# Stationary halves at 14 turns of placement and pass order, in the transposed projections of a decoder trunk

## The chip, the core and the metric

One core of one Trainium2 chip runs the whole kernel. The metric is device microseconds (us) of one execution, from the runs' own times. Before the change the median of two runs is 2431.1 us (2430.3 to 2431.9).

## What is computed

A two-layer decoder trunk on one sequence of 256 tokens with width 2048, in float32: a retention layer, a gated ConvFFN, a sliding-window attention layer, a second ConvFFN, and a last RMSNorm. The reference, cut to its order:

```python
def reference(x, ...):
    h = x
    for i in range(DEPTH):                      # DEPTH = 2
        j = i // N_MIXERS
        hn = rmsnorm(h, norm_mix_g[i])
        if i % N_MIXERS == 0:
            h = h + retention(hn, ret_w_in[j], ret_w_out[j])
        else:
            h = h + sliding_window_attention(hn, att_w_qkv[j], att_b_qkv[j], att_sinks[j], att_w_out[j])
        hn = rmsnorm(h, norm_ffn_g[i])
        h = h + conv_ffn(hn, ffn_w_up[i], ffn_conv_w[i], ffn_conv_b[i], ffn_w_down[i])
    return rmsnorm(h, final_norm_g)
```

Nearly all of the work is `hn @ w` with weights that are read once from HBM: 456 MB of them.

## The kernel before, in words

**Weights come in units.** A unit (`Unit`) is one transfer of 1 MB: up to 2048 words in each of the 128 partitions, for instance 8 chunks of 128 weight rows by 256 columns, or 4 chunks by 512. SP issues the transfers into `raw` (L146 in the printed functions below), some units ahead. ACT rounds `raw` to the high half `hi` (L161), VectorE subtracts to get the low half `lo` (L162), both in pieces of 1024 words. `hi` and `lo` have four buffers each, and each buffer is 2048 + 64 words long, so that the data may start up to 64 words into it. A product of a weight and an activation is built from three products of halves: high by high, high by low and low by high.

**Two kinds of product.** In the output projections and the values (`products`, L256 to L258), the weights are the moving operand and the activations the stationary one: three passes of 512 columns (256 in one unit kind) into the same PSUM tile, each with its own 128 by 128 stationary tile. In the transposed projections (`products_tr`, L267 and L269: queries, keys, and the up projections of both FFNs), the weights are stationary. One *chunk* there is four passes: the stationary tiles H0 and H1 (the two 128-column halves of `hi`) are each applied to the moving tile `xT` in 512 columns (high and low half of the activations side by side), then L0 and L1 (of `lo`) are each applied to the first 256 columns of the same tile. H0 and L0 add into PSUM bank 0 of the group, H1 and L1 into bank 1. Sixteen chunks (2048 rows) make a group, which is then evicted.

**Passes and loads.** Each pass needs its stationary tile loaded (LDWEIGHTS, shown as PEld) before it begins; the load of a pass runs while the pass before it streams its moving tile. A pass of 512 columns is a long cover for the next load, a pass of 256 columns a short one.

**Where the tiles lie.** All `xT` tiles and all `hi`/`lo` buffers start at multiples of 64 words (256 bytes). In units that have a transposed group, `hi` and `lo` start `ASIDE` = 48 words into their buffers, in the others at 0. So the distance from the start of the moving tile to the start of the tile that is being loaded is, modulo 64 words, 48 for every load in a transposed group. In the `products` units it is 0, and 16 in the three units that hold the attention's keys and values together (moving at 48, stationary at 0).

**Order.** `run_main` goes over the units, and in a unit over groups and chunks; after each chunk it lets the splits run ahead (`split_ahead`) and runs pending small tasks (evictions, scores, transposes), whose PE instructions then stand between chunks. PE executes in the order written.

Of the kernel before, what the change touches and what calls it, by code (L numbers as in the profile page):

```python
# [10 lines left out]
F32R = mybir.dt.float32r  # L11
# [5 lines left out]
P = 128  # L17
D = 2048
S = 256
# [12 lines left out]
AHEAD = 3  # L32
# [13 lines left out]
RAW = 2  # L46
SPLIT = 1024

ASIDE = 48
F_CUTS = [0, 14, 28, NF]  # L50
START = (1, 1, 2, 2, 2)

# [57 lines left out]
class Kernel:  # L110
# [37 lines left out]
    def splits(self, i):  # L148

        u = self.units[i]  # L150
        nc = self.nc
        w = u.n * u.cols
        at = ASIDE if any(g.tr for g in u.groups) else 0
        u.hi, u.lo = (
            self.wp.tile([P, 2048 + 64], F32R, tag=tag, name=tag, bufs=AHEAD + 1)[:, at : at + w]
            for tag in ("hi", "lo")
        )
        for c in range(0, w, SPLIT):
            e = min(c + SPLIT, w)
            raw, hi, lo = (x[:, c:e] for x in (u.raw, u.hi, u.lo))  # L160
            nc.scalar.copy(out=hi, in_=raw)  # L161
            nc.vector.tensor_tensor(out=lo, in0=raw, in1=hi.bitcast(F32), op=ALU.subtract)  # L162
            yield e / w
# [29 lines left out]
    def run_main(self):  # L193
        for i, u in enumerate(self.units):
            self.load_to(i + AHEAD + RAW)
            self.split_ahead(i)
            for g in u.groups:
                if g.ps is None:
                    if g.begin:
                        g.begin()  # L200
                    g.ps = self.banks(g)
            if u.groups[0].by_token:
                break
            for j, g in enumerate(u.groups):
                c0 = sum(x.cols for x in u.groups[:j])
                for kk, ch in enumerate(u.chunks):
                    sl = slice(kk * u.cols + c0, kk * u.cols + c0 + g.cols)
                    if g.tr:
                        self.products_tr(g, u.hi[:, sl], u.lo[:, sl], u.act[ch])
                    else:  # L210
                        for t in range(2):
                            out = g.ps[t] if g.apart else g.ps[:, t]
                            self.products(g, out, t, u.hi[:, sl], u.lo[:, sl], u.act[ch])
                    g.seen += 1
                    self.step += g.cols / 512
                    if g.seen == g.total:
                        g.done(g)
                    share = (self.step - u.at) / u.steps
                    self.split_ahead(i, share - 1e-6)
                    self.run_tasks()  # L220
        self.run_by_token(self.units[i:])
        while self.tasks:
            self.step += 1
            self.run_tasks()
# [32 lines left out]
        nc.tensor.matmul(out, lhsT=ah, rhs=lo, start=False, stop=False)  # L257
        nc.tensor.matmul(out, lhsT=al, rhs=hi, start=False, stop=last)  # L258

    def products_tr(self, g, hi, lo, act):  # L260

        nc = self.nc
        first, last = g.seen == 0, g.seen == g.total - 1
        both = act.rearrange("p x s -> p (x s)")
        tiles = [(g.ps[:, i], slice(i * P, (i + 1) * P)) for i in range(2)]
        for out, sl in tiles:
            nc.tensor.matmul(out, lhsT=hi[:, sl], rhs=both, start=first, stop=False)  # L267
        for out, sl in tiles:
            nc.tensor.matmul(  # L269
                out[:, :S], lhsT=lo[:, sl], rhs=act[:, 0], start=False, stop=last  # L270
            )


    def transposes(self, ps, ins):
# [683 lines left out]
```

## Time and profile before

| | before |
|---|---|
| median of the runs | 2431.1 us |
| the profiled execution's own time | 2431.45 us |
| its span, first to last instruction | 2429.3 us |
| PE busy | 2413.0 us (99%) |
| weight loads (PEld) busy | 2060.6 us (85%) |
| VectorE busy | 1554.9 us (64%) |
| ScalarE busy | 1224.6 us (50%) |
| mean granted TensorE clock | 0.999 |
| mean DMA rate | 189 GB/s |

Busy times of PE are unions of overlapping instructions: a pass of 512 columns lasts 393 ns from its first to its modelled last moment, but the next one starts long before that. What a pass costs is therefore read from starts: the start of the next pass minus its own start. The timeline view merges equal instructions that follow each other into one row with xN, so that a row "L267 ... x2" followed by "L269 ... x2" shows when the H pair and the L pair began.

### The profile page before, as it was taken

How to read it: one execution, taken by the hardware profiler on the slowest of the kernel's cores; microseconds unless marked ns; L12 is line 12 of the kernel's file. 1: busy time of each engine (PE TensorE's matmuls, PEld its weight loads, DVE VectorE, ACT ScalarE, POOL GpSimd, SP SyncE). 2: the span in 40 equal slices, each digit the busy share in tenths (PEclk: the TensorE clock that was granted, in tenths of full speed). 3: DMA queues.
4: the chain of work that ended last, by engine and by line, in shares of the span. 5: the costliest groups of instructions: out<-in, count | busy, mean ns of one | idle time of the engine just before them, and what ended most of it. 6: DMA issues, size and time to landing. Idle time of an engine off the chain costs nothing.

```text
span 2429.3 us, 31370 instructions
## 1 busy us (share of the span) xinstructions
PE 2413.0 (99%) x12676; PEld 2060.6 (85%) x12676; DVE 1554.9 (64%) x2104; ACT 1224.6 (50%) x1782; POOL 29.2 (1%) x37
## 2 busy tenths in 40 slices
PE   8999999999999999999999999999999999999998
PEld 7888888888888888888888888888888888888887
DVE  6555555554556775677577756876777477657774
ACT  6444344344445553555355545765555355535553
POOL 3000000000000000000000000000000000000000
PEclk9999999999999999999999999999999999999999
DMA  8655555555554555555555555445454555554553
GB/s 287 213 187 180 192 181 186 185 188 182 182 191 168 199 185 194 192 192 183 197 192 195 194 182 195 182 156 193 174 194 174 207 191 191 190 207 175 195 200 126
DMA packets 68977, 460.27 MB, mean 189 GB/s; under 512 B 8032, under 2 KB 9184, under 8 KB 16736
## 3 DMA queue, kind: packets, MB, share of 16 engines
q1 hardware_dynamic: 68544, 457.23, 52.7%
q8 instruction: 99, 1.62, 0.3%
q10 hardware_dynamic: 288, 1.05, 0.1%
q14 instruction: 46, 0.38, 0.0%
HBM read 456.15 MB, written 2.10 MB: 189 GB/s over the span
## 4 chain that ended last, share of the span: by engine, by line
PE 97%; DMA 1%; issue 1%; POOL 0%; DVE 0%; ACT 0%; SPq 0%; POOLq 0%; DVEq 0%; ACTq 0%
PE mm L267 33%; PE mm L269 17%; PE mm L256 13%; PE mm L258 12%; PE mm L257 12%; PE po L256 2%; PE po L258 2%; PE po L257 2%; PE po L393 1%; PE ms L276 1%; PE ms L679 1%; PE ms L503 0%; POOL acc L309 0%; DMA h<-in_xT 0%; DVE lo L162 0%
## 5 line engine op out<-in xcount | busy, mean ns | idle before, releaser
L162 DVE TENSOR_TENSOR lo<-raw,hi 128x1024 fp32r<-128x1024 f32 (+1 forms) x849 | 1018.4, 1219 | 612.3 <-ACT hi L161 611.9
L161 ACT CAST hi<-raw 128x1024 fp32r<-128x1024 f32 (+1 forms) x849 | 857.8, 1042 | 522.5 <-PE mm L258 332.3
L267 PE MATMUL mm<-xT,hi 128*128 128x512 f32 x3552 | 1107.9, 393 | 6.2 <-DVE xT L323 6.2
L269 PEld LDWEIGHTS mm<-xT,lo 128*128 128x128 f32 x3552 | 667.3, 188 | 150.3 <-DVE lo L162 3.1
L269 PE MATMUL mm<-xT,lo 128*128 128x256 f32 x3552 | 702.2, 279 | 1.1 <-DVE lo L162 1.0
L267 PEld LDWEIGHTS mm<-xT,hi 128*128 128x128 f32 x3552 | 540.5, 188 | 11.7 <-ACT hi L161 6.2
L256 PE MATMUL mm<-hi,zT 128*128 128x512 f32 x688 | 268.3, 390 | 0.0
L258 PE MATMUL mm<-hi,zT 128*128 128x512 f32 x688 | 267.7, 389 | 0.0
L257 PE MATMUL mm<-lo,zT 128*128 128x512 f32 x688 | 267.7, 389 | 0.0
L601 DVE SCALAR_TENSOR_TENSOR cv<-u,cw,cv 128x255 f32<-128x255 f32 x344 | 158.3, 481 | 6.1
L256 PE MATMUL mm<-hi,yT 128*128 128x512 f32 x384 | 153.3, 399 | 0.0
L258 PEld LDWEIGHTS mm<-hi,zT 128*128 128x128 f32 x688 | 129.1, 188 | 27.0
L257 PEld LDWEIGHTS mm<-lo,zT 128*128 128x128 f32 x688 | 129.2, 188 | 26.5
L256 PEld LDWEIGHTS mm<-hi,zT 128*128 128x128 f32 x688 | 129.1, 188 | 26.4
L258 PE MATMUL mm<-hi,yT 128*128 128x512 f32 x384 | 149.8, 390 | 0.0
L257 PE MATMUL mm<-lo,yT 128*128 128x512 f32 x384 | 149.7, 390 | 0.0
L378 ACT COPY u<-mm 128x512 f32<-128x512 f32 x86 | 50.4, 586 | 183.7 <-PE mm L269 183.7
L379 DVE TENSOR_TENSOR u<-mm,u 128x512 f32<-128x512 f32 x86 | 59.5, 692 | 93.2 <-ACT u L378 93.2
L594 ACT ACTIVATE cv<-u,cw 128x256 f32<-128x256 f32 x172 | 94.2, 595 | 48.7 <-DVE u L388 48.7
L611 ACT CAST zT<-cv 128x256 fp32r<-128x256 f32 x86 | 34.9, 406 | 156.2 <-DVE cv L609 156.2
L256 PE MATMUL mm<-hi,xT 128*128 128x512 f32 (+1 forms) x288 | 109.1, 379 | 0.0
L258 PE MATMUL mm<-hi,xT 128*128 128x512 f32 (+1 forms) x288 | 108.6, 377 | 0.0
(118 smaller groups left out, 1784.1 us busy)
## 6 DMA issues: line engine op xcount, KB each, us to landing
raw<-in_up SPq DMA_DIRECT2D x172, 1024.0 KB, 4.7
raw<-in_ret_in SPq DMA_DIRECT2D x94, 1024.0 KB, 4.8
raw<-in_dn SPq DMA_DIRECT2D x72, 1024.0 KB, 4.8
raw<-in_ret_out SPq DMA_DIRECT2D x32, 1024.0 KB, 4.7
raw<-in_qkv SPq DMA_DIRECT2D x20, 1024.0 KB, 4.7
raw<-in_att_out SPq DMA_DIRECT2D x14, 1024.0 KB, 4.7
raw<-in_dn SPq DMA_DIRECT2D x16, 512.0 KB, 3.2
raw<-in_dn SPq DMA_DIRECT2D x8, 768.0 KB, 4.3
```

The lines of the kernel that those rows point to most:

```text
L161: nc.scalar.copy(out=hi, in_=raw)
L162: nc.vector.tensor_tensor(out=lo, in0=raw, in1=hi.bitcast(F32), op=ALU.subtract)
L256: nc.tensor.matmul(out, lhsT=ah, rhs=hi, start=first, stop=False)
L257: nc.tensor.matmul(out, lhsT=ah, rhs=lo, start=False, stop=False)
L258: nc.tensor.matmul(out, lhsT=al, rhs=hi, start=False, stop=last)
L267: nc.tensor.matmul(out, lhsT=hi[:, sl], rhs=both, start=first, stop=False)
L269: nc.tensor.matmul(out[:, :S], lhsT=lo[:, sl], rhs=act[:, 0], start=False, stop=last)
L378: nc.scalar.copy(out=x, in_=g.ps[:, :, S:])
L379: nc.vector.tensor_tensor(out=x, in0=g.ps[:, :, :S], in1=x, op=ALU.add)
L594: nc.scalar.activation(out=c[:, half], in_=u[:, half], func=AF.Identity, scale=w[:, 2:3], bias=w[:, 3:4])
L601: nc.vector.scalar_tensor_tensor(out=c[:, half, d:], in0=u[:, half, : S - d], scalar=w[:, 2 - d : 3 - d], in1=c[:, half, d:], op0=ALU.mult ...
L611: nc.scalar.copy(out=z[:, 0], in_=s)
```

## The change

`CASES` holds 14 triples: the offset of `hi` in its buffer, the offset of `lo`, and the order of the four passes. Unit number i takes triple i modulo 14; units without a transposed group keep offset 0 and have no use for the order.

- 7 triples keep `hi` at 48 and put `lo` at 0, 8, 16, 24, 32, 40 or 56.
- 4 keep `lo` at 48 and put `hi` at 0, 16, 32 or 56.
- 3 keep both at 48 and take another order: H0 H1 L1 L0, H0 L0 L1 H1, or H0 L1 L0 H1.

In the first and the last chunk of a group the old order H0 H1 L0 L1 is kept, because these carry the start and stop marks of the accumulation.

```diff
-ASIDE = 48
+CASES = [(48, x, "H0H1L0L1") for x in (0, 8, 16, 24, 32, 40, 56)]
+CASES += [(x, 48, "H0H1L0L1") for x in (0, 16, 32, 56)]
+CASES += [(48, 48, x) for x in ("H0H1L1L0", "H0L0L1H1", "H0L1L0H1")]
...
-        at = ASIDE if any(g.tr for g in u.groups) else 0
+        *at, u.order = CASES[i % len(CASES)]
+        if not any(g.tr for g in u.groups):
+            at = (0, 0)
         u.hi, u.lo = (
-            self.wp.tile([P, 2048 + 64], F32R, tag=tag, name=tag, bufs=AHEAD + 1)[:, at : at + w]
-            for tag in ("hi", "lo")
+            self.wp.tile([P, 2048 + 64], F32R, tag=tag, name=tag, bufs=AHEAD + 1)[:, x : x + w]
+            for tag, x in zip(("hi", "lo"), at)
         )
...
-                        self.products_tr(g, u.hi[:, sl], u.lo[:, sl], u.act[ch])
+                        self.products_tr(g, u.hi[:, sl], u.lo[:, sl], u.act[ch], u.order)
...
-        tiles = [(g.ps[:, i], slice(i * P, (i + 1) * P)) for i in range(2)]
-        for out, sl in tiles:
-            nc.tensor.matmul(out, lhsT=hi[:, sl], rhs=both, start=first, stop=False)
-        for out, sl in tiles:
-            nc.tensor.matmul(
-                out[:, :S], lhsT=lo[:, sl], rhs=act[:, 0], start=False, stop=last
-            )
+        if first or last:
+            order = CASES[0][2]
+        for n in range(0, 8, 2):
+            i = int(order[n + 1])
+            out, sl = g.ps[:, i], slice(i * P, (i + 1) * P)
+            if order[n] == "H":
+                nc.tensor.matmul(out, lhsT=hi[:, sl], rhs=both, start=first, stop=False)
+            else:
+                nc.tensor.matmul(
+                    out[:, :S], lhsT=lo[:, sl], rhs=act[:, 0], start=False, stop=last
+                )
```

What that makes of the loads can be counted in the built program by its addresses. A load is named by the pass that streams meanwhile and the tile that is loaded (HL: an H pass streams, an L tile is loaded), and by the distance of the two modulo 64 words. Before, all of them are at 48.

| load | 0 | 8 | 16 | 24 | 32 | 40 | 48 | 56 | not at 48 |
|---|---|---|---|---|---|---|---|---|---|
| HH (under 512 columns) | 136 | | 136 | | 128 | | 1242 | 128 | 528 |
| HL (under 512 columns) | 118 | 118 | 120 | 132 | 132 | 144 | 868 | 144 | 908 |
| LL (under 256 columns) | 118 | 118 | 120 | 132 | 132 | 144 | 868 | 144 | 908 |
| LH (under 256 columns) | 126 | | 129 | | 120 | | 1212 | 124 | 499 |

The orders show in PE's sequence of instructions. First place: the first unit of the second retention head (early in the program), queries, chunks one to four; `mm` is the PSUM tile, `hi_1085` and `lo_1086` the unit's halves, `po` a retention output that stands between. Before:

```order
L267 MATMUL mm_1178<-xT_118,hi_1085 128x512 x2
L269 MATMUL mm_1178<-xT_118,lo_1086 128x256 x2
L267 MATMUL mm_1178<-xT_120,hi_1085 128x512 x2
L269 MATMUL mm_1178<-xT_120,lo_1086 128x256 x2
L393 MATMUL po_1193<-v_1039,sch_952 128x512 x3
L267 MATMUL mm_1178<-xT_128,hi_1085 128x512 x2
L269 MATMUL mm_1178<-xT_128,lo_1086 128x256 x2
```

The same place after the change (lines 276 and 278 are the H and the L pass there):

```order
L276 MATMUL mm_1178<-xT_118,hi_1085 128x512 x2
L278 MATMUL mm_1178<-xT_118,lo_1086 128x256 x2
L276 MATMUL mm_1178<-xT_120,hi_1085 128x512
L278 MATMUL mm_1178<-xT_120,lo_1086 128x256 x2
L276 MATMUL mm_1178<-xT_120,hi_1085 128x512
L402 MATMUL po_1193<-v_1039,sch_952 128x512 x3
L276 MATMUL mm_1178<-xT_128,hi_1085 128x512
L278 MATMUL mm_1178<-xT_128,lo_1086 128x256 x2
```

From the second chunk on, the two L passes stand between the two H passes; the work between the chunks stays where it was. Second place: a unit of the first FFN's up projection, whose turn is H0 L0 L1 H1, in the middle of it, after the change:

```order
L276 MATMUL mm_5578<-xT_5128,hi_5481 128x512
L278 MATMUL mm_5578<-xT_5128,lo_5482 128x256 x2
L276 MATMUL mm_5578<-xT_5128,hi_5481 128x512
L276 MATMUL mm_5578<-xT_5143,hi_5481 128x512
L278 MATMUL mm_5578<-xT_5143,lo_5482 128x256 x2
L276 MATMUL mm_5578<-xT_5143,hi_5481 128x512
```

The H1 of one chunk and the H0 of the next now follow each other, so that the passes still come in twos: two of 512 columns, two of 256.

## Rows read from the trace of the kernel before

**Rows 1.** The page: span, PE's busy time, granted clock in 40 slices.

```profile
span 2429.3 us, 31370 instructions
...
PE 2413.0 (99%) x12676; PEld 2060.6 (85%) x12676; DVE 1554.9 (64%) x2104; ACT 1224.6 (50%) x1782; POOL 29.2 (1%) x37
...
PEclk9999999999999999999999999999999999999999
```

**Rows 2.** Waits of PE: engine, line, waited for: total us, times, longest.

```profile
PE mm L267 <- DVE xT L323: 6.2, 1, 6.2
PE mm L269 <- DVE lo L162: 1.0, 3, 0.5
PE ms L352 <- POOL acc L309: 0.4, 1, 0.4
```

**Rows 3.** The page's chain that ended last: shares by engine, then by line.

```profile
PE 97%; DMA 1%; issue 1%; POOL 0%; DVE 0%; ACT 0%; SPq 0%; POOLq 0%; DVEq 0%; ACTq 0%
PE mm L267 33%; PE mm L269 17%; PE mm L256 13%; PE mm L258 12%; PE mm L257 12%; PE po L256 2%; PE po L258 2%; PE po L257 2%; PE po L393 1%; PE ms L276 1%; PE ms L679 1%; PE ms L503 0%; POOL acc L309 0%; DMA h<-in_xT 0%; DVE lo L162 0%
```

**Rows 4.** The page's costliest groups: count | busy us, mean ns | idle before.

```profile
L267 PE MATMUL mm<-xT,hi 128*128 128x512 f32 x3552 | 1107.9, 393 | 6.2 <-DVE xT L323 6.2
L269 PEld LDWEIGHTS mm<-xT,lo 128*128 128x128 f32 x3552 | 667.3, 188 | 150.3 <-DVE lo L162 3.1
L269 PE MATMUL mm<-xT,lo 128*128 128x256 f32 x3552 | 702.2, 279 | 1.1 <-DVE lo L162 1.0
```

**Rows 5.** PE's timeline in a steady up projection: start us, us, instruction, count.

```profile
895.16 0.62 PE L267 MATMUL mm<-xT,hi 128*128 128x512 f32 x2
895.62 0.39 PE L269 MATMUL mm<-xT,lo 128*128 128x256 f32 x2
895.85 0.62 PE L267 MATMUL mm<-xT,hi 128*128 128x512 f32 x2
896.30 0.40 PE L269 MATMUL mm<-xT,lo 128*128 128x256 f32 x2
896.54 0.62 PE L267 MATMUL mm<-xT,hi 128*128 128x512 f32 x2
...
904.82 0.62 PE L267 MATMUL mm<-xT,hi 128*128 128x512 f32 x2
```

**Rows 6.** The same in a steady down projection: two starts, 84 passes apart.

```profile
1150.56 0.39 PE L256 MATMUL mm<-hi,zT 128*128 128x512 f32 x1
...
1169.60 0.39 PE L256 MATMUL mm<-hi,zT 128*128 128x512 f32 x1
```

**Rows 7.** Timeline, attention's values: 12 passes of 256 columns, distance 16.

```profile
1465.27 0.28 PE L256 MATMUL mm<-hi,xT 128*128 128x256 f32 x1
...
1466.68 0.60 PE L276 MATMUL ms<-ident,h 128*128 128x128 f32 x4
```

**Rows 8.** Timeline, L pairs before other work: distance 0, 0, 40.

```profile
82.68 0.39 PE L269 MATMUL mm<-xT,lo 128*128 128x256 f32 x2
82.90 0.63 PE L393 MATMUL po<-v,sch 128*128 128x512 f32 x2
...
1136.02 0.40 PE L269 MATMUL mm<-xT,lo 128*128 128x256 f32 x2
1136.26 0.39 PE L256 MATMUL mm<-hi,zT 128*128 128x512 f32 x1
...
753.48 0.41 PE L269 MATMUL mm<-xT,lo 128*128 128x256 f32 x2
753.72 0.60 PE L276 MATMUL ms<-ident,h 128*128 128x128 f32 x4
```

**Rows 9.** Timeline, the first four passes of a down projection.

```profile
905.51 0.40 PE L256 MATMUL mm<-hi,zT 128*128 128x512 f32 x1
...
906.44 0.39 PE L257 MATMUL mm<-lo,zT 128*128 128x512 f32 x1
```

**Rows 10.** Groups by line, 800 to 890 us (offset 48), then 905 to 970 (offset 0).

```profile
L162 DVE TENSOR_TENSOR lo<-raw,hi 128x1024 fp32r<-128x1024 f32 x33 | 40.3, 1220 | 11.4 <-ACT hi L161 11.4
...
L161 ACT CAST hi<-raw 128x1024 fp32r<-128x1024 f32 x32 | 32.6, 1044 | 0.0
...
L162 DVE TENSOR_TENSOR lo<-raw,hi 128x1024 fp32r<-128x1024 f32 x24 | 28.6, 1221 | 27.7 <-ACT hi L161 27.7
L161 ACT CAST hi<-raw 128x1024 fp32r<-128x1024 f32 x24 | 24.3, 1052 | 35.5 <-PE mm L258 35.5
```

**Rows 11.** Busy us by engine, 800 to 890: PE, PEld, DVE, ACT, POOL; clock, DMA.

```profile
800.00:890.00 90.00, 90.00 (x523) 79.19 (x523) 69.67 (x100) 50.72 (x73) 0.00 (x0) 1.00 0.54 191
```

**Rows 12.** Timeline near the start: an L pair whose tiles came late.

```profile
15.18 0.50 PE L269 MATMUL mm<-xT,lo 128*128 128x256 f32 x2 [0.52 <-DVE lo L162]
15.52 0.63 PE L267 MATMUL mm<-xT,hi 128*128 128x512 f32 x2
```

More of the change, by code (lines that the diff above doesn't have):

```diff
@@ L258, in products, with products_tr @@
         nc.tensor.matmul(out, lhsT=al, rhs=hi, start=False, stop=last)
-    def products_tr(self, g, hi, lo, act):
+    def products_tr(self, g, hi, lo, act, order):
         nc = self.nc
```

## The prediction

> **What bounds the kernel now.** [...] The chain that ended last is PE for 97%, and half of it is the two lines that the change touches, L267 with 33% and L269 with 17% [rows 3]. So transfers, splits and evictions are hidden, and the time is the sum of PE's passes. The change keeps every pass; it can move the time only by the length of a pass, which is the time to the start of the next.
>
> That length is read from starts. In a steady up projection the H pair of one chunk begins at 895.16 and that of the fourteenth chunk after it at 904.82: 9.66 / 14 = 690 ns a chunk [rows 5]. Inside, the H pair takes 0.46 and 0.45 us by turns and the L pair 0.23 and 0.24, so on average an H pass takes 227.5 ns and an L pass 117.5 (each to a few ns, since starts are printed to 10 ns). There are 3552 / 2 = 1776 such chunks [rows 4]; they hold 1776 x 0.690 = 1225 us, half of the span.
>
> How short could a chunk be? In a steady down projection, where every load has a pass of 512 columns as cover and the distance is 0, 84 passes take 1169.60 - 1150.56 = 19.04 us, or 226.7 ns each [rows 6]. That is 0.4427 ns a column, and a chunk of 512 + 512 + 256 + 256 columns would take 680 ns. So a chunk loses 10 ns to all that may collide in it, and 1776 of them lose 17.8 us. No placement and no order can win more than that as long as this floor holds: 0.7% of the time.
>
> [...]
>
> **The change, part by part.**
>
> *Loads under short passes (LL and LH).* [...] 908 LL loads and 499 LH loads leave distance 48, 1407 in all. The trace of before has short passes at three other distances. At 16, twelve passes of 256 columns take 1466.68 - 1465.27 = 1.41 us, 117.5 ns each: no different from 48 [rows 7]. At 0, an L pair whose second load belongs to the next work takes 0.22 us in one place and 0.24 in another; at 40 it takes 0.24 [rows 8]. So what I see lies between 0.22 and 0.24 for a pair that takes 0.235 on average at 48. As an upper bound each such load puts its pair at the slower 0.24: 1407 x 5 ns = 7.0 us. As a lower bound nothing (a gain is bounded below, for all parts together). I take the middle, +3.5 us, because two of the three places with a single odd load show 0.24.
>
> *Loads under long passes (HL and HH).* 908 + 528 = 1436 of them leave 48. They have 227 ns of cover, and at distance 0 passes of that length take 226.7 [rows 6], against 227.5 here. The worst that I find for 512 columns is just behind a border between two kinds of work: four passes from 905.51 to 906.44, 232.5 each [rows 9]. The bounds are therefore -0.8 x 1436 = -1.1 us and 5 x 1436 = +7.2 us; I take 0, since the long run of 84 is nearer to this place than a border is.
>
> *The three orders.* 3 of 14 units keep both halves at 48. Counted round the chunk border, each order has one HH, one HL, one LL and one LH load as before, so no pass gets a shorter cover. What is new is that H0 and L0 (or L1 and H1) follow each other into the same PSUM bank; in the down projection three passes in a row go to the same bank at 226.7 ns [rows 6], so this costs 0. L0 is needed one H pass (227 ns) earlier than before, in the second to last-but-one chunk of a group only. The low halves are ready well ahead: after the first 24 us PE never waits for them [rows 2] (the longest of the three waits is that of [rows 12]). I cost it at 0; if that cover were gone, a unit would pay at most 227 ns in its first chunk, with 222 units / 14 x 2 = 32 of them 7 us.
>
> *ACT and VectorE.* Both write and read at new offsets. At offset 48 the subtraction takes 1220 ns and the cast 1044, at offset 0 it is 1221 and 1052 [rows 10]: the offset costs nothing that shows. Were it dearer, VectorE is the nearer to its limit, with 69.67 of 90 us busy in an up projection [rows 11], so a split could grow by half (33 x 1220 ns x 0.5 = 20 us in that stretch) before PE would feel it. Transfers, buffers and semaphores stay.
>
> *Sum.* The profiled execution took 2431.45 us (2429.3 span, 2.15 around it; the median of the runs shown is 0.35 lower, which is nothing here). 2431.45 + 3.5 + 0 + 0 = 2434.95, so **2435 us**, a change of 0.15%.
>
> **The rivals.**
>
> *Nothing happens (B).* The distance plays no part, and the 10 ns come from elsewhere, for instance from the switch between long and short passes, which stays. For it: distances 0, 16, 40 and 48 look alike to 10 ns a pair. Against it: the alternation of 0.23 and 0.24 shows that loads and passes do interact, and each new distance may shift it. Time: 2431 us. [...]
>
> *A gain (C).* Some of the new distances, or of the orders, bring chunks to the 680 ns floor. All 14 turns change something, so at most 1776 chunks x 10 ns = 17.8 us: 2413.7. More likely some of the turns win and others lose; a third of it would be 2425. For it: one L pair at distance 0 took 0.22 [rows 8]. Against it: the other pair at 0 took 0.24.
>
> *A collision (D), the other side.* At a distance that before doesn't have in a steady run, the load can't proceed while the pass streams, and the next pass starts late. The place would be short passes at odd multiples of 8 words: LL at 8, 24, 40, 56 (118 + 132 + 144 + 144 = 538) and LH at 56 (124), 662 loads. Price: where an L pair's tiles came late, so that a load had no cover, the pair took 0.34 instead of 0.235 us [rows 12], 105 ns more. 662 x 105 ns = 69.5 us, so 2501 us. It counts as slower from 2% = 48.6 us on, that is from 73 ns per such load. For it: in the stretch of [rows 11] loads are in flight 79.19 of 90 us, so there is no room to hide a longer one. Against it: the one such distance that the trace has, 40, costs no more than 0.24 a pair [rows 8].
>
> **How the numbers follow.** My forecast (A), a small loss of 1 to 11 us (2432 to 2442, the forecast's own terms up to about three quarters of their upper bounds 7.0 + 7.2), has a chance of 0.55; B (2429 to 2432) 0.20; C below that 0.13, of which 0.08 above 2424; D 0.12, of which 0.05 is a partial collision that stays within 2%, below 2480 us, and 0.07 is over it. A range from 2424 to 2450 us leaves out about 0.05 of C and 0.11 of D. Its low end is a little under half of the largest possible gain, its high end holds both upper bounds (2431.45 + 7.0 + 7.2 = 2445.7) and the start of a partial collision. 2% is about what a measurement of this kernel can tell from no change. Faster by over 2% would need 48.6 us where the floor leaves 17.8: 0.01. Slower by over 2% is D in full: 0.07. Within 2%: 0.92.
>
> **What the profile after would show.** If A is right, a chunk in a steady up projection takes between 685 and 705 ns in every unit, by turns of 14, with the L pairs between 0.22 and 0.25 us; units with one of the three orders stay at 690; the waits of PE and the durations of the split stay as they were; the granted clock stays at its upper level. If C is right, some turns show chunks near 680. If D is right, the L pairs of the turns with `lo` at 8, 24, 40 or 56 stand out with up to 0.34 us, and the others don't. What would make all of this wrong is an effect that 10 ns rows of single pairs can't show: one that needs several loads at the same distance in a row, as the changed units have in each of their 8 chunks.

## The result, and the profile after

The changed kernel takes 2443.9 us (2443.5 to 2444.4) against 2431.1: a ratio of 1.0053 with an interval of 1.0036 to 1.0069, 12.8 us slower. The prediction was 2435 with a range of 2424 to 2450, and 0.92 for a change within 2%.

The page of the changed kernel, the lines that answer to [rows 1] and [rows 3] and to the two matmul groups of [rows 4] (lines 276 and 278 are the H and the L passes now):

```profile
span 2442.2 us, 31370 instructions
...
PE 2426.0 (99%) x12676; PEld 2067.1 (85%) x12676; DVE 1555.2 (64%) x2104; ACT 1224.8 (50%) x1782; POOL 29.2 (1%) x37
...
PEclk9999999999999999999999999999999999999999
...
PE 97%; DMA 1%; issue 1%; POOL 0%; DVE 0%; ACT 0%; SPq 0%; POOLq 0%; ACTq 0%
...
L276 PE MATMUL mm<-xT,hi 128*128 128x512 f32 x3552 | 1116.5, 395 | 6.3 <-DVE xT L332 6.2
...
L278 PE MATMUL mm<-xT,lo 128*128 128x256 f32 x3552 | 707.8, 280 | 1.1 <-DVE lo L168 1.0
```

The span grew by 12.9 us and PE's busy time by 13.0, at the same instruction count and granted clock (0.999 in both), while VectorE (+0.3) and ScalarE (+0.2) stayed. These busy times overlap and their ends are modelled, so the cost of a pass is counted from starts, in ns, over all passes of the trace: the H passes hold 7.6 us more, the L passes 5.5, and everything else 0.1 less. PE's waits, by engine, line, what it waited for, total us, times and longest, answer to [rows 2] and changed by 0.1 us at most:

```profile
PE mm L276 <- DVE xT L332: 6.2, 1, 6.2
PE mm L278 <- DVE lo L168: 1.0, 2, 0.5
PE ms L361 <- POOL acc L318: 0.3, 1, 0.3
```

So no wait took the time: the passes themselves became longer. PE's timeline in the first FFN's up projection shows where. Each row is the first H pair of a unit, for six units that follow each other (start us, duration of the merged row, instruction, count); a unit has 8 chunks:

```profile
1029.69 0.63 PE L276 MATMUL mm<-xT,hi 128*128 128x512 f32 x2
...
1035.29 0.63 PE L276 MATMUL mm<-xT,hi 128*128 128x512 f32 x2
...
1040.84 0.62 PE L276 MATMUL mm<-xT,hi 128*128 128x512 f32 x2
...
1046.38 0.62 PE L276 MATMUL mm<-xT,hi 128*128 128x512 f32 x2
...
1052.04 0.63 PE L276 MATMUL mm<-xT,hi 128*128 128x512 f32 x2
...
1057.69 0.63 PE L276 MATMUL mm<-xT,hi 128*128 128x512 f32 x2
```

The first five are the turns with `hi` at 48 and `lo` at 8, 16, 24, 32 and 40; the sixth row ends the last of them. Their lengths are 5.60, 5.55, 5.54, 5.66 and 5.65 us, or 700, 694, 692.5, 707.5 and 706 ns a chunk; before, it was 690 [rows 5]. Inside the turn with `lo` at 32, the L pairs take 0.24 to 0.25 us and the H pairs 0.46 to 0.47:

```profile
1046.85 0.41 PE L278 MATMUL mm<-xT,lo 128*128 128x256 f32 x2
1047.09 0.63 PE L276 MATMUL mm<-xT,hi 128*128 128x512 f32 x2
1047.55 0.41 PE L278 MATMUL mm<-xT,lo 128*128 128x256 f32 x2
1047.80 0.63 PE L276 MATMUL mm<-xT,hi 128*128 128x512 f32 x2
```

The trace's starts in ns give the same for all turns. Here and below, a pass is the time from its start to the next pass's start and a chunk four of them; the first 40 us and those with other work or a wait between (a pass over 300 ns, a chunk over 720) are left out of the means. Before, a chunk is 690.3 ns in this count. After:

| `hi` / `lo` at, order | ns a chunk | | `hi` / `lo` at, order | ns a chunk |
|---|---|---|---|---|
| 48 / 0 | 698.4 | | 0 / 48 | 693.8 |
| 48 / 8 | 700.2 | | 16 / 48 | 693.7 |
| 48 / 16 | 694.1 | | 32 / 48 | 704.7 |
| 48 / 24 | 693.5 | | 56 / 48 | 699.7 |
| 48 / 32 | 706.2 | | H0 H1 L1 L0 | 693.3 |
| 48 / 40 | 706.8 | | H0 L0 L1 H1 | 691.5 |
| 48 / 56 | 698.0 | | H0 L1 L0 H1 | 692.4 |

No turn is below 690.3. Summed over the chunks counted here, the excess is 12.4 us, nearly all of the 12.8 us. By the kind of the load and its distance, in ns a pass (the first column is the kernel before, all at 48):

| load | 48, before | 48 | 0 | 8 | 16 | 24 | 32 | 40 | 56 |
|---|---|---|---|---|---|---|---|---|---|
| HH | 227.9 | 229.7 | 232.1 | | 226.8 | | 236.0 | | 235.3 |
| HL | 230.5 | 230.4 | 233.7 | 233.3 | 235.5 | 228.7 | 232.7 | 238.6 | 234.5 |
| LL | 116.7 | 118.2 | 116.7 | 118.0 | 118.0 | 118.1 | 123.8 | 118.6 | 117.5 |
| LH | 115.5 | 116.9 | 115.8 | | 118.2 | | 118.3 | | 114.8 |

The column for 48 matters as much as the others: passes whose own load kept its distance became longer too. Of the 12.8 us that these means make over all counted passes, 7.7 lie on passes whose load left 48 and 5.1 on passes whose load stayed there (HH 2.2, LH 1.7, LL 1.3, HL -0.1). So a pass's length depends on the loads of its neighbours as well as on its own.

The table also tells which tile counts. In the four turns that move `hi` alone, the H1 passes have a moved tile of their own and load an L tile that is still at 48; they take 230.2 ns, against 230.5 before. The H0 passes of the same turns, which load the moved H1, take 226.8 to 236.0. So a long pass changes mainly by the tile that is loaded under it, not by its own.

### The profile page after: what moved, and what is told of

It reads as the page before. It is cut to its first block, busy times and chain, and to the rows that moved or that the text cites. A ratio compares the mean times of both kernels' runs of the same rounds, so it can differ in the third digit from the quotient of the medians.

```text
span 2442.2 us, 31370 instructions
## 1 busy us (share of the span) xinstructions
PE 2426.0 (99%) x12676; PEld 2067.1 (85%) x12676; DVE 1555.2 (64%) x2104; ACT 1224.8 (50%) x1782; POOL 29.2 (1%) x37
## 4 chain that ended last, share of the span: by engine, by line
PE 97%; DMA 1%; issue 1%; POOL 0%; DVE 0%; ACT 0%; SPq 0%; POOLq 0%; ACTq 0%
PE mm L276 33%; PE mm L278 17%; PE mm L262 12%; PE mm L263 12%; PE mm L264 12%; PE po L262 2%; PE po L264 2%; PE po L263 2%; PE po L402 1%; PE ms L285 1%; PE ms L688 1%; PE ms L512 0%; POOL acc L318 0%; DVE lo L168 0%; DMA h<-in_xT 0%
## 5 line engine op out<-in xcount | busy, mean ns | idle before, releaser
L276 PEld LDWEIGHTS mm<-xT,hi 128*128 128x128 f32 x3552 | 546.5, 188 | 13.1 <-ACT hi L167 6.5
L262 PE MATMUL mm<-hi,xT 128*128 128x512 f32 (+1 forms) x288 | 109.1, 379 | 0.0
L263 PE MATMUL mm<-lo,xT 128*128 128x512 f32 (+1 forms) x288 | 108.6, 377 | 0.0
```

The costliest lines, as they stand in the source:

```text
L262: nc.tensor.matmul(out, lhsT=ah, rhs=hi, start=first, stop=False)
```

## The experiments

The theory under test: what lengthens a pass is the distance, modulo 64 words, between the tile that streams and the tile that is loaded under it. Rivals: the change of placement from unit to unit (1) and the place of a half in its own buffer (2). Later come two theories for what is left over the floor of 680 ns: the mix of long and short passes (S) and the PSUM bank (B; not the prediction's rival B).

### One placement everywhere: `lo` at 32

```diff
-CASES = [(48, x, "H0H1L0L1") for x in (0, 8, 16, 24, 32, 40, 56)]
-...
+CASES = [(48, 32, "H0H1L0L1")]
```

> hi at 48 and lo at 32 in every transposed unit, old order, no turns. Theory (each pass is lengthened by the distance, modulo 64 words, between the tile that streams and the tile that is loaded under it, wherever it stands): the turns of the changed kernel with this placement took about 706.5 ns a chunk against 690.2 before, so 1776 x 16.3 ns = 29 us more, 2460 us. Rival 1 (the loss comes from changing the placement from unit to unit, which makes passes and loads find their rhythm anew): nothing changes from unit to unit here, so 2431 us.

2452.7 us, ratio 1.0091 (1.0076 to 1.0106): 21.9 us slower. Rival 1 falls, since nothing turns here. But it is three quarters of the 29 us expected: a chunk takes 703.2 ns, not 706.2. The same distances run in another rhythm: in the turned kernel this unit's chunks mostly take 706 or 707 ns one after the other, here in most units a chunk of 709 to 711 ns is followed by one of 692 to 701. And the H0 passes, whose load is still at 48, take 232.2 ns against 227.9 before: 4.3 of the 12.9 ns of a chunk's loss lie there. The distance of a load sets that there is a loss, but alone neither its size nor the pass that shows it.

### Both halves at 0, and then xT moved by 16

```diff
-ASIDE = 48
+ASIDE = 0
```

> hi and lo both at 0 in every unit, old order. Theory of distances: loads at distance 0 took in the changed kernel 4.2 (HH), 3.2 (HL), 0 (LL) and 0.3 (LH) ns more than at 48, together 7.7 ns a chunk or 13.7 us: 2445 us. Rival 1 (turns): 2431 us. Rival 2 (what counts is where in its buffer a half lies, for its writers ACT and VectorE or for the read of it, not the distance to the moving tile): also about 2445 us; the next kernel tells it from the theory.

2441.6 us, ratio 1.0045 (1.0030 to 1.0060), 10.9 us slower; 696.6 ns a chunk. The same edit, with the moving tile moved as well:

```diff
-            x = self.acts.tile([P, 2, S], F32R, tag="xT", name="xT", bufs=NC)
+            x = self.acts.tile([P, 2 * S + 64], F32R, tag="xT", name="xT", bufs=NC)
+            x = x[:, 16 : 16 + 2 * S].rearrange("p (x s) -> p x s", x=2)
...
-        at = ASIDE if any(g.tr for g in u.groups) else 0
+        at = 16 if u.act is self.xT and not u.groups[0].tr else 0
```

> hi and lo at 0 in the transposed units as in the kernel with both at 0, but every xT tile begins 16 words into its buffer, so that all distances in transposed groups are 48 again modulo 64 words; in the products that use xT as stationary tile the weights begin at 16, so that those stay at 0. Theory of distances: 2431 us, as before. Rival 2 (the place of a half in its own buffer): as with both at 0, about 2445 us. Rival 1: 2431 us.

2430.9 us, ratio 1.0001 (0.9991 to 1.0010), and 690.5 ns a chunk. PE's timeline in the same up projection, two H pairs 26 chunks apart, first with both halves at 0 and then with xT moved as well:

```profile
884.73 0.63 PE L267 MATMUL mm<-xT,hi 128*128 128x512 f32 x2
...
902.84 0.63 PE L267 MATMUL mm<-xT,hi 128*128 128x512 f32 x2
```

```profile
884.73 0.62 PE L267 MATMUL mm<-xT,hi 128*128 128x512 f32 x2
...
902.66 0.62 PE L267 MATMUL mm<-xT,hi 128*128 128x512 f32 x2
```

That is 18.11 against 17.93 us, or 697 against 690 ns a chunk. `hi` and `lo` stand at 0 in both kernels, and the distance alone gives the 10.7 us back. Rival 2 falls. This is the experiment that shows the cause: what counts is where the streaming tile and the tiles loaded meanwhile lie relative to each other, not where either lies by itself. How the two disturb each other inside the chip, no run shows.

### More turns

```diff
+CASES = [(x, x, "H0H1L0L1") for x in (0, 8, 16, 24, 32, 40, 56)]
+CASES += [(x, 48, "H0H1L0L1") for x in (8, 24, 40)]
+CASES += [(16, 24, "H0H1L0L1"), (24, 16, "H0H1L0L1")]
+CASES += [(48, 48, "H0L0H1L1"), (48, 48, "H0L1H1L0")]
+CASES += [(16, 16, "H0L0H1L1"), (24, 24, "H0L0H1L1"), (0, 0, "H0L0H1L1")]
```

> Another set of 17 turns: hi and lo both at 0, 8, 16, 24, 32, 40 and 56; hi at 8, 24 or 40 with lo at 48; (16, 24) and (24, 16); orders H0 L0 H1 L1 and H0 L1 H1 L0 at 48 and, of the first, at 16, 24 and 0. Theory of distances with one price for each kind of load and distance: from the changed kernel's loads a chunk at (0, 0) takes 698, (16, 16) 698.5, (32, 32) 711, (56, 56) 702, (16, 24) 692 ns; hi at 24 and 40 are open, and if hi and lo have the same good places, 24 is near 692 and 40 near 707. If short passes are what limits, orders that alternate H and L, which leave no load of an L tile under an L pass, come nearer to 680 ns; if not, they stay at 690 or above.

2448.9 us in its one execution. In ns a chunk: both at 0 696.6, 8 701.6, 16 696.6, 24 704.7, 32 701.3, 40 700.6, 56 706.5; `hi` at 8, 24, 40 with `lo` at 48: 702.1, 704.9, 699.0; (16, 24) 698.7, (24, 16) 700.7. Single alternation at 48: 703.1 and 700.1; at 16 704.6, at 24 695.4, at 0 704.9. The expected values hit for (0, 0) and (16, 16) within 2 ns, and miss by 10 for (32, 32), 4.5 for (56, 56) and 7 for (16, 24); nor has `hi` the same good places as `lo`, since `hi` at 24 took 704.9 and not 692, and at 40 699.0 and not 707. A price list with one entry for each kind of load and distance doesn't add up. That (0, 0) has 696.6 here, in turns, and 696.6 alone is one more word against rival 1. And alternating orders, which leave no L load under an L pass, are longer at 48, 16 and 0, not nearer to 680; at 24 the alternation is the shorter of the two (695.4 against 704.7). So what an order costs depends on the distance too.

### The orders alone

```diff
+CASES = [(48, 48, x) for x in ("H0H1L1L0", "H0L0L1H1", "H0L1L0H1")]
...
-            order = CASES[0][2]
+            order = "H0H1L0L1"
```

> Both halves at 48 in every transposed unit; only the three new orders (H0 H1 L1 L0, H0 L0 L1 H1, H0 L1 L0 H1) by turns, old order in the first and last chunk of a group. Theory (the placements carry the loss, orders of passes in twos cost nothing): chunks with these orders took 691 to 692 ns in the changed kernel against 690.2 before, so about 1 ns x 1776 = 2 us, 2433 us. Rival (the orders carry the 12.8 us, in 3 of 14 units): 14/3 x 12.8 = 60 us more, 2491 us.

2432.9 us, ratio 1.0006 (0.9997 to 1.0015): no difference that can be told, and nothing near 2491. The loss belongs to the placements.

### The products at 32

```diff
-        at = ASIDE if any(g.tr for g in u.groups) else 0
+        at = ASIDE if any(g.tr for g in u.groups) else 32
```

> The transposed units as before (48); in all other units, whose weights stream and whose activations are loaded, hi and lo begin at 32 instead of 0, so that 4752 passes of 512 columns have a load at distance 32 under them. Theory (any load at such a distance lengthens the pass over it, also under a long pass in a run of long passes): loads at 32 under 512 columns took 233 (HL) to 236 ns (HH) in the changed kernel against 226.7 at 0 here, so 6 to 9 ns x 4752 = 29 to 44 us more, 2460 to 2475 us. Rival (long passes lose only because short ones beside them start late; by itself a pass of 227 ns covers any load, as the prediction costed it at 0): 2431 us.

2456.7 us, ratio 1.0105 (1.0090 to 1.0120), 25.8 us slower; the transposed units are unchanged. PE's timeline in the down projection that [rows 6] show at 226.7 ns a pass (start, duration, instruction):

```profile
1149.97 0.39 PE L256 MATMUL mm<-hi,zT 128*128 128x512 f32 x1
...
1152.75 0.40 PE L256 MATMUL mm<-hi,zT 128*128 128x512 f32 x1
```

Twelve passes take 2.78 us, 231.7 ns each; over all of them the mean rises from 227.3 to 232.6. So a long pass is lengthened by a load at 32 even where there are only long passes, with a cover of 227 ns for every load. The rival falls at this distance, and with it the prediction's 0 for loads under long passes. The 25.8 us lie a little below the expected 29 to 44.

### Fewer changes between long and short passes

Two chunks are taken together, four H passes and then four L passes; in the second kernel a whole unit is, 16 and 16.

```diff
                     if g.tr:
-                        self.products_tr(g, u.hi[:, sl], u.lo[:, sl], u.act[ch])
+                        self.highs(g, u.hi[:, sl], u.act[ch])
+                        held.append((u.lo[:, sl], u.act[ch], g.seen == g.total - 1))
+                        if (kk + 1) % 2 == 0 or kk + 1 == u.n:    # 8 in the second
+                            self.lows(g, held)
```

> Both halves at 48; two chunks of a unit are taken together: four H passes, then four L passes, half as many changes between long and short passes. Theory S (what is left of a chunk over the floor of 680 ns comes from the changes between long and short passes; orders that change four times a chunk instead of twice took 700 to 705 ns against 690): 690 - 5 = 685 ns a chunk, 9 us less, 2422 us. Theory of distances alone: the same distances, so the same time, 2431 us.

> As in the kernel with fours, but all H passes of a group's chunks in a unit, then all its L passes: 16 and 16 in units of 8 chunks, 8 and 8 in units of 4. Theory S: 690 - 8.75 = about 681 ns a chunk, 15 us less, 2416 us. Theory of distances alone: 2431 us. If instead the loads under short passes are what costs, a run of 16 of them shows it: more than 2431 us.

2433.9 us (ratio 1.0013, 1.0004 to 1.0023) and 2434.2 (1.0013, 1.0004 to 1.0023). Theory S falls: no gain, rather 3 us of loss. PE's timeline of the second, with runs of 16 (start, duration, instruction, count):

```profile
1003.11 3.84 PE L267 MATMUL mm<-xT,hi 128*128 128x512 f32 x16
1006.79 1.98 PE L275 MATMUL mm<-xT,lo 128*128 128x256 f32 x16
1008.60 3.82 PE L267 MATMUL mm<-xT,hi 128*128 128x512 f32 x16
1012.26 2.05 PE L275 MATMUL mm<-xT,lo 128*128 128x256 f32 x16
1014.14 1.09 PE L267 MATMUL mm<-xT,hi 128*128 128x512 f32 x4
```

The H runs take 3.68 and 3.66 us, 229 ns a pass; the L runs 1.81 and 1.88, 113 and 117.5 ns. In the means it is 229.5 for an H pass while an H tile is loaded and 115.9 for an L pass while an L tile is, so a chunk is 691 ns, as in twos. At distance 48 the 10 ns over the floor stay in all three groupings by twos, fours and sixteens.

### The PSUM bank

In `by_bank` all H0 passes of a unit come first, then all H1, all L0, all L1; with both halves at 48, and at 0:

```diff
+        for i in range(2):
+            for hi, lo, act, seen in held:
+                self.nc.tensor.matmul(
+                    g.ps[:, i], lhsT=hi[:, i * P : (i + 1) * P],
+                    rhs=act.rearrange("p x s -> p (x s)"), start=seen == 0, stop=False,
+                )
+        for i in range(2):
+            for hi, lo, act, seen in held:
+                self.nc.tensor.matmul(
+                    g.ps[:, i, :S], lhsT=lo[:, i * P : (i + 1) * P], rhs=act[:, 0],
+                    start=False, stop=seen == g.total - 1,
+                )
```

> As in the kernel that takes all H passes of a unit and then all its L passes, at 48, but sorted by PSUM bank as well: all H0, then all H1, all L0, all L1. Theory B (what is left over the floor at 48, and what distance 0 costs the H passes though it costs the products nothing, comes from changing the PSUM bank with each pass; the products stay three passes in a bank): 680 ns a chunk, so 16 us less than the kernel sorted by H and L, 2418 us. Theory of distances alone: the loads are at 48 as there, 2434 us.

> The same order by PSUM bank with both halves at 0. Theory B: also 680 ns a chunk, 2418 us. Theory of distances alone, with the H passes at 0 taking 233 to 235 ns as with both halves at 0 in the old order: 5 to 7 ns more for each of two H passes a chunk and 1 ns less for each L pass, so about 10 us over the one at 48, 2444 us.

2449.4 us (ratio 1.0075, 1.0058 to 1.0091) and 2461.3 (1.0122, 1.0107 to 1.0137). Theory B falls: at 48 the passes are as without the sorting by bank (229.3 and 115.8 ns). That this kernel is 15 us slower than the one sorted by H and L alone has other causes. Its waits show the first: with all passes of a unit issued at its end, the attention's transposes come before their operands are ready.

```profile
PE ms L280 <- DVE pr L714: 9.9, 4, 3.1
PE mm L266 <- DVE xT L327: 6.6, 1, 6.6
PE ms L280 <- DVE soft L691: 2.8, 4, 0.7
```

In the kernel sorted by H and L the same waits are these; so 10.7 of the 15 us are waits (9.9 + 2.8 against 1.1 + 0.9):

```profile
PE ms L283 <- DVE pr L717: 1.1, 2, 0.6
PE ms L283 <- DVE soft L694: 0.9, 2, 0.4
```

The granted clock shows the second. Around the end of two waits of 3 us it reads 0.50 for 3.4 us each time. The first of the two (stretch, its length, busy us and instructions of PE, PEld, DVE, ACT and POOL, then the granted clock, DMA share and GB/s):

```profile
1511.10:1514.50 3.40, 3.06 (x10) 2.63 (x11) 3.37 (x15) 2.19 (x7) 0.00 (x0) 0.50 0.00 0
```

In the kernel sorted by H and L the clock does not fall there; over the whole execution its mean is 0.999, against 0.997 here. If PE goes at half its pace there, an estimate from the 0.50, the two stretches, 6.8 us together, cost up to 3.4 us; with the waits that is 14.1 of the 15 us. The kernel at 0 has the same two stretches and the same waits, to within 0.2 us, so they drop out of the next comparison.

Between the two kernels sorted by bank, the one at 0 is 11.9 us slower, where 10 were expected from distances. Its timeline:

```profile
1003.48 2.08 PE L272 MATMUL mm<-xT,lo 128*128 128x256 f32 x16
1005.39 3.82 PE L266 MATMUL mm<-xT,hi 128*128 128x512 f32 x16
1009.04 2.08 PE L272 MATMUL mm<-xT,lo 128*128 128x256 f32 x16
1010.95 3.82 PE L266 MATMUL mm<-xT,hi 128*128 128x512 f32 x16
```

An H run takes 3.65 us, 228 ns a pass; an L run 1.91 us, 119.4 ns. With H and L in twos at 0, the H passes took 233.0 (HH) and 233.2 (HL) and the L passes 114.7 (LL) and 116.0 (LH). The sum of a chunk is the same in both, 2 x 228.8 + 2 x 119.4 = 696.4 by the means against 696.6. So the same loss shows on the short passes when they stand in runs, and on the long ones when they stand in twos. That fits a late start that moves on to the neighbours, as the loads that stayed at 48 do, but no run shows a single start move; and the runs at 0 differ from the twos in the sorting by bank too, which changed no pass at 48 (229.5 and 115.9 without it, 229.3 and 115.8 with it).

The other side of theory B, the products with a change of bank at each pass:

```diff
-                        for t in range(2):
-                            out = g.ps[t] if g.apart else g.ps[:, t]
-                            self.products(g, out, t, u.hi[:, sl], u.lo[:, sl], u.act[ch])
+                        self.products_alt(g, u.hi[:, sl], u.lo[:, sl], u.act[ch])
...
+        for n, (x, rhs) in enumerate(((0, hi), (0, lo), (1, hi))):
+            for t in range(2):
...
```

> Transposed units as before; the products (weights stream, distance 0) change the PSUM bank with each pass: for each of the three products of halves, first the first, then the second 128 tokens. Two passes that follow each other then stream the same tile, as in the transposed groups. Theory B: passes of 226.7 ns come to the 230 to 235 of the H passes, 3 to 8 ns x 4500 = 14 to 37 us more, 2445 to 2468 us. Theory of distances alone: all loads are at 0 modulo 64 words as before, 2431 us.

2431.3 us, ratio 0.9999 (0.9990 to 1.0008), and 227.3 ns a pass as before. How often the bank changes played no part that shows in either kind of product.

### Single alternation

```diff
+CASES = [(48, 48, "H0L0H1L1")]
```

> Both halves at 48 in every transposed unit, order H0 L0 H1 L1 except in the first and the last chunk of a group: long and short passes alternate singly, all loads at 48. Theory of distances alone: 2431 us. Theory C (a load that comes late under a short pass is paid by the pass after it, and a single long pass between two short ones has to take up more than a pair has): the turns with this order took 703 ns a chunk in the second set of turns, 13 ns x 1550 = 20 us more, 2451 us.

2451.8 us, ratio 1.0086 (1.0069 to 1.0103): 20.9 us slower at unchanged distances, as expected from the turns; a chunk takes 702.7 ns. This order cost nearly as much as `lo` at 32 everywhere (21.9 us). Theory C is only in line with this; it says why by an argument, and the same loads, taken two by two, cost 690.3 a chunk.

## Why the prediction came out as it did

**The bound: right.** PE's passes made the time, before and after: PE is 97% of the chain that ended last in both. The waits stayed within 0.1 us, the busy times of VectorE and ScalarE within 0.3 us, and the clock at 0.999. The whole change is found in the lengths of the transposed passes: by starts 7.6 us on the H passes and 5.5 on the L passes.

**The floor and the sign of the gain: right.** None of the 31 combinations of placement and order that ran in turns took a chunk under 690 ns on average, and the 680 ns from [rows 6] were never reached. Rival C had 0.13 and got nothing.

**Loads under short passes: about right.** The sum has +3.5 us for 1407 loads, with an upper bound of 7.0; the L passes whose load left 48 hold 2.4 us more (LL 1.75, LH 0.6). That a pass needs its tile loaded before it begins, as the kernel's description has it, the records of these loads don't show. By the starts in ns of the kernel before, a load starts 3 ns after the pass over it and lasts 188 ns (medians); under a long pass it ends 38 to 40 ns before its own pass starts, under a short one 72 to 74 ns after. When a tile has to be in place, no run shows.

**Loads under long passes: the term that was mis-sized.** The sum has 0 for 1436 loads, with bounds of -1.1 and +7.2; the H passes whose load left 48 hold 5.3 us more (HL 3.0, HH 2.3). The value came from the long run of products at distance 0 [rows 6]. Two things were wrong with it. It spoke for one distance, and at another (32) the same products lose 5 ns a pass. And even for distance 0 it didn't speak for H passes that stand between short ones: those took 233 ns, while in runs they took 228.8 and the L passes paid instead. The row just behind a border, 232.5 [rows 9], which the prediction used as its upper bound, was nearer: 1436 x 5 ns = 7.2 us. Whether those four passes are long for the same reason, no run shows.

**Loads that stay at 48: the term that was missing.** The sum counts loads that leave 48 and gives the others nothing, without a reason. Their passes hold 5.1 us more, two fifths of the change. That a pass can become longer when only the loads beside its own change was not in the prediction, which priced each load by itself.

**One reading.** From starts printed to 10 ns the prediction took 227.5 ns for an H pass and 117.5 for an L pass. The starts in ns give 229.2 and 116.1, and the H passes that load an L tile stood at 230.5 before the change. So about half of the 10 ns that a chunk loses over the floor already lay on long passes, the ones that the prediction took to cover their loads. Two counts are off by a little and move nothing: 227 units have a transposed group, not 222, and four hold the attention's keys and values, not three.

**The orders: right.** Costed at 0; alone they gave a ratio of 1.0006 with 1 in its interval. The chunks of the three turns took 691.5 to 693.3 ns. The unit in which L0 is needed earlier shows no wait.

**The rivals.** B (nothing happens) fell by its own evidence: rows of single pairs printed to 10 ns couldn't tell 0, 16, 40 and 48 apart, but means over some hundred passes do. The prediction named this as what would make it wrong. Of D, the place was wrong: LL loads at odd multiples of 8 took 117.5 to 118.6 ns, the dearest was 32 with 123.8, and no kind of load made an L pair come near 0.34 us on average.

**The size.** The change is 12.8 us instead of 3.9, three times what the sum gave, and 2443.9 lies 2 us over the forecast's own range (2432 to 2442). It lies inside the whole range, which held both upper bounds and some more. That it is a small loss follows from the bound and the floor; that the upper end was wide enough is in part luck, since 5.1 of the 12.8 us fell where neither upper bound had anything.

## What to carry to other kernels

In this kernel, with PE busy for 99% of the span, the address of a stationary tile relative to the tile that streams while it is loaded was a cost of its own, up to 17 ns in a chunk of 690 (706.8 with `lo` at 40). In another kernel with a busy PE it can be looked for in the same way, by turning through placements and reading starts from the trace. A price for such an effect is taken from a place with the same neighbours: at distance 0, long passes in a run took 228.8 ns and long passes between short ones 233. The passes beside the changed ones belong in the sum too. And averages over many passes decide; single pairs printed to 10 ns hid an effect of 0.5% of the whole time here.

## What the runs showed that was not expected

A pass of 512 columns with a cover of 227 ns for the load still lost 5.3 ns to a load at distance 32 (227.3 to 232.6), in a run of such passes. At equal distances a chunk can settle in different rhythms: 706 to 707 ns flat, or 709 to 711 and 692 to 701 by turns, with `lo` at 32, and 690 or 700 by the chunk's place in its unit with `hi` at 0 and `lo` at 48. At distance 48, alternating long and short passes singly cost 12 ns a chunk against the same passes in twos; at 24 it gained 9. What sets the rhythm, and why a distance of 0 costs the products nothing that shows (227.3, against 232.6 at 32) but does cost the transposed passes (696.6 ns a chunk against 690.5), stays open: neither the PSUM bank nor the grouping of long and short passes removed the difference.
